# An encoder block on one core: whole-width sums and a new load order in the opening, v stores from ScalarE's queue, and another order of key evictions at the switch of heads

## The chip, the cores and the metric

The kernel runs on one core of one Trainium2 chip, in one launch. The metric is the device time of a launch in microseconds (us). Engines are called by their short names in the rows: PE is TensorE, PEld its weight loads, DVE VectorE, ACT ScalarE, POOL GpSimd, and SP SyncE, which here only issues transfers.

## What is computed

One encoder block on a sequence of 1024 positions with 1024 channels, in fp32. The conditioning vector c gives six vectors of shift, scale and gate through one matrix of 1024 x 6144:

```python
ada = jax.nn.silu(c) @ w_ada[i] + b_ada[i]
shift1, scale1, gate1, shift2, scale2, gate2 = [t[:, None, :] for t in jnp.split(ada, 6, axis=-1)]
h = rmsnorm(x, g_mix[i]) * (1 + scale1) + shift1
proj = h @ w_in[i]
qa, ka, va, qb, kb, vb, ga, gb = jnp.split(proj, split_at, axis=-1)
oa = mixture_of_dilations(heads(qa, N_HEADS_DIL), heads(ka, N_HEADS_DIL), heads(va, N_HEADS_DIL), rel_bias)
ob = neighbourhood_attention_2d(heads(qb, N_HEADS_NA), heads(kb, N_HEADS_NA), heads(vb, N_HEADS_NA), na_rpb[i])
merged = jax.nn.sigmoid(ga) * ya + jax.nn.sigmoid(gb) * yb
x = x + gate1 * (merged @ w_out[i])
```

`ya` and `yb` are oa and ob times a branch matrix each. Then follow a second norm, a feed-forward part with a depthwise convolution of width 3 and 2816 gated channels, and a final norm. There are eight dilated heads (three dilations each, merged by their denominators) and eight neighbourhood heads (a window of 8 x 16 on a grid of 16 x 64), all of width 64. The change touches the first norm, its modulation, the products for v, and the eviction of keys.

## The kernel before

**Products in three parts.** Every fp32 matrix product is made of three fp32r matmuls: an operand a is copied by ACT into its rounded high part, and DVE or POOL subtract that from a to give the low part. PE then adds high times high, high times low and low times high (`product`, L84 to L86). So each weight tile needs one ACT copy (`split`, L57) and one subtraction (L61), and each result that is used again as an operand needs both again: keys come out of PSUM as `ks` (ACT, L370) and `kl` (DVE, L374), softmax weights, transposed by PE into `T`, as `th` (ACT, L666) and `tl` (DVE, L667).

**The opening** (L437 to L530) is written in the order in which the engines are to run it; a manual schedule holds for all engines up to the attention. Positions go in two halves of 512; x of half 0 is loaded first. Its squares are summed over channel tiles on ACT and DVE (`total`, L452), and PE sums over the partitions by matmuls with a column of ones into `pcol` (`add_sums`, L98). DVE and ACT make r, the reciprocal root, of it; PE spreads r over the partitions into `pbc` (L111), and x is multiplied by it. At the same time comes the modulation of half of the channels that a "piece" needs: w_ada is loaded in columns of 512, each as four transfers of two row tiles. Of the eight row tiles, PE sums some directly by matmuls of one output column with c as the moving operand (`ada_sums`, L160, tile `pada`), and DVE accumulates the others (`ada_rows`, L174 and L176), with the accumulated rest summed by PE against ones. `piece_bias` (L293, L295) makes shift and scale of it; ACT then makes `h` (L229) and DVE its low part (L231). A loop over four pieces q of two channel tiles each does this and the products of one q and one k tile (`qk_products`, L310) and of v (`v_parts`, L320). Between the sums stand dummy matmuls on ones (`warm`, L236, out `pv`, in `om`), which compute nothing that is used.

**The v stage** (L538 to L606). For six further column groups of w_ada (j = 4 to 9) rows come in pairs (`pair_load`, L135, seven in flight); DVE sums them (L551, L553), and two steps later PE sums over partitions into `pada` and L167 adds the bias. Between these stand the v products, 128 positions by 512 columns each (`v_wide`, L279 to L281). A table `row_ends` says after which step how many pairs have been summed. `v_out` copies a product from PSUM on ACT (`vs`, two buffers, L286) and stores it to DRAM by a transfer on SP's queue (L287), from which the attention loads it again in another order. The first step without v products splits the v weights of the neighbourhood heads (L57, L61 with `vwh`, `vwl`).

**The attention** (L1074 to L1100) has 100 slots. Slots up to 63 hold turns of the dilated heads, from 64 on those of the neighbourhood heads. A slot runs on PE, in this order: O products (`th`, `tl` times v, L844), filler products of w_in (L84 to L86, one k step each), transposes T (L781, L827), filler, score products S, filler, W, filler. Each `fill` step also calls `catch_up(550)`, which hands out "asides" of a deque: evictions of the filler products, copies of v, splits. An aside is one or two closures with a cost; the first runs on ACT, the second on DVE, in an in-order stream of each engine. `k_evict` makes the asides of a key product: for a neighbourhood pair of heads one aside per head, ACT's copy `ks`, then DVE's `kl` (a cost of 750 for each). L658 and L659 are the two steps of the softmax (DVE, then ACT), L701 and L702 the eviction of O into `u`.

Transfers complete on eight semaphores that SP and ACT use in turn, so that the ninth issue waits until the first has landed.

Of the kernel before, what the change touches and what calls it, by code (L numbers as in the profile page):

```python
# [18 lines left out]
D = 1024  # L19
# [10 lines left out]
def hybrid_encoder(tc, xT, c, w_ada, small, w_in, p1_bias, p23_bias, na_bias, ln2_mult, ident, w_br, w_out,  # L30
# [62 lines left out]
    qkpool = tc.alloc_tile_pool(name="qk", bufs=4)  # L93

# [189 lines left out]
    def v_out(br, st, p, c0=0):  # L284
        vs = work.tile([128, 512], FT, name="vs", bufs=2)[:, :p.shape[-1]]
        act.activation(vs, p, AF.Copy)  # L286
        sp.dma_start((va_s, vb_c)[br][st * 128:st * 128 + 128, c0:c0 + p.shape[-1]], vs)  # L287
# [17 lines left out]
    def qk_products(ks):  # L305
        for k in ks:
            mhi, mlo = h[0, k]
            for x_, (part, m) in enumerate(((0, mhi), (1, mhi), (0, mlo))):
# [48 lines left out]
    def k_evict(br, qk, hf, p, later=at_once):  # L357
# [26 lines left out]
        for i in range(2 if br else 0):  # L384
            later(750, lambda i=i: one((i,)), lambda i=i: two((i,)))
# [33 lines left out]
    with tc.manual_schedule(engines={e.engine for e in (sp, act, dve, pool, pe)}):  # L419
# [5 lines left out]
        v_raw = [qkpool.tile([128, KT, 128], FT, name="kl") for _ in range(2)]  # L425
        half_load(v_raw, (8, 9), 0)
        wt.append(ada_load(1))
        half_load(qk_raw, (0, 4), 1)
        half_load(v_raw, (8, 9), 1)
        wt.append(ada_load(2))  # L430
# [15 lines left out]
        warm(35, idle, True)  # L446
# [6 lines left out]
        pcol = ps_n.tile([128, KT], FT, name="pcol")  # L453
        add_sums(pcol, total, True, True)
        warm(3, idle, True)
        pa = ada_sums([(wt[0][0], cs[:, 0:1])], stop=False)
        r = wpool.tile([128, KT], FT, name="rs", bufs=2)[:, :4]
        dve.tensor_scalar(r, pcol[:, :4], 1.0 / D, EPS, OP.mult, OP.add)
        act.activation(r, r, AF.Sqrt)
        ada_rows(wt[0], acc, range(3, 4), 3, 7)  # L460
# [3 lines left out]
        warm(3, idle, True)  # L464
        ada_sums([(wt[0][1], cs[:, 1:2])], pa, stop=False)
        warm(4, idle, True)
        ada_sums([(wt[0][2], cs[:, 2:3])], pa, stop=False)
        warm(2, idle, True)
        pbs = early.tile([128, 512], FT, name="mt", bufs=3)
        act.activation(pbs, pb, AF.Copy)  # L470
        ada_rows(wt[0], acc, range(4, 8), 3, 7)
        for k in range(2):
            dve.tensor_tensor(x[0][k], x[0][k], pb, OP.mult)
        ada_sums([(wt[0][7], ones)], pa)
        warm(5, idle, True)
        for q in range(4):
            ks = range(2 * q, 2 * q + 2)
            piece_bias(q, pa)
            if q == 0:
                for k in range(2, 4):  # L480
                    dve.tensor_tensor(x[0][k], x[0][k], pb, OP.mult)
                stage = [ps_n.tile([128, 512], FT, name=n) for n in ("pcol", "pbc")]
            low = [scaled(x[0][k], k) for k in ks]
            if q == 0:
                v_split(v_raw, (pool, pool), slice(0, 4), v_w[0])
                for k in range(4, 8):
                    pool.tensor_tensor(x[0][k], x[0][k], pbs, OP.mult)
# [4 lines left out]
            steps = (range(q + 1, 4), range(4, 5), range(5, 7)) if q else (range(0), range(2), range(2, 6))  # L492
# [5 lines left out]
            if q < 2:  # L498
                ada_rows(wt[q + 2], acc, range(q + 2), 0, 6)
# [6 lines left out]
            qk_products(ks)  # L506
# [1403 lines left out]
```

## Time and profile before

| What | us |
|---|---|
| three timed runs | 1501.80, 1496.16, 1500.61 |
| their median | 1500.61 |
| the profiled execution | 1498.67 |
| its span, first to last instruction | 1496.8 |
| PE busy | 1474.4 |
| DVE busy | 939.0 |
| ACT busy | 773.6 |
| POOL busy | 760.6 |

The rows of the profile are one execution; 1.87 us of its time lie outside of the span. The granted clock of PE was full (0.998 in the mean). A row of the timeline names start, duration, engine, line of the kernel, operation, the tile written and those read, and in brackets the idle time of the engine just before it and what ended that. A matmul on plain fp32 (sums, dummies, transposes of r) is recorded as two.

### The profile page before, as it was taken

The numbers are of one execution on the slowest core, as the hardware profiler recorded it, in microseconds if no ns is written. First come the engines' busy times: TensorE is split into PE (matmuls) and PEld (weight loads), VectorE is DVE, ScalarE is ACT, GpSimd is POOL, SyncE is SP. The second block draws the span as 40 slices with busy tenths as digits, with TensorE's granted clock in tenths as the row PEclk, the third lists the DMA queues.
The fourth block names the chain that finished last, engine by engine and source line by source line (L and its number), as shares of the span: only waits on it lengthen the run. The fifth ranks groups of instructions, "written<-read, shape, count | busy, mean of one in ns | idle before, by whom it ended". The sixth has DMA issues, their size and how long they took to land.

```text
span 1496.8 us, 21659 instructions
## 1 busy us (share of the span) xinstructions
PE 1474.4 (98%) x7664; PEld 1251.9 (84%) x7664; DVE 939.0 (63%) x1763; ACT 773.6 (52%) x1442; POOL 760.6 (51%) x633
## 2 busy tenths in 40 slices
PE   9999999999999999999999999999999999999997
PEld 8888888889798998888888778888888888877887
DVE  7683446465555665556515897666666667886865
ACT  4531666666655666653345464444444447474542
POOL 3031332434234454512268668766666776978811
PEclk9999999999999999999999999999999999999999
DMA  9577332444645555577544313222222233542313
GB/s 371 183 277 268 88 99 68 143 114 129 170 144 145 144 160 166 172 243 260 194 153 143 104 43 141 85 85 85 85 83 84 71 136 116 197 148 64 104 41 113
DMA packets 117301, 210.29 MB, mean 140 GB/s; under 512 B 42788, under 2 KB 55716, under 8 KB 117156
## 3 DMA queue, kind: packets, MB, share of 16 engines
q1 hardware_dynamic: 116632, 208.57, 43.4%
q8 instruction: 60, 0.98, 0.3%
q14 instruction: 49, 0.40, 0.1%
q10 hardware_dynamic: 560, 0.33, 0.1%
HBM read 163.58 MB, written 42.66 MB: 138 GB/s over the span
## 4 chain that ended last, share of the span: by engine, by line
PE 81%; DVE 5%; POOL 5%; DMA 4%; issue 2%; ACT 2%; SPq 0%; DVEq 0%; POOLq 0%; ACTq 0%
PE pj L84 10%; PE pj L86 10%; PE pj L85 10%; PE pj L1308 10%; PE pj L1307 10%; PE pj L1306 10%; PE pj L402 3%; PE O L1013 2%; DMA wraw<-w_down 2%; PE T L1000 1%; PE S L978 1%; POOL wsl L61 1%; PE pv L279 1%; PE pv L281 1%; PE pv L280 1%
## 5 line engine op out<-in xcount | busy, mean ns | idle before, releaser
L61 POOL TENSOR_TENSOR wlo<-wraw,whi 128x512 fp32r<-128x512 f32 (+1 forms) x84 | 106.1, 1284 | 144.8 <-ACT whi L57 129.8
L84 PE MATMUL pj<-h,whi 128*128 128x512 f32 x432 | 178.1, 412 | 0.4 <-DVE kl L374 0.4
L86 PE MATMUL pj<-h,wlo 128*128 128x512 f32 x432 | 169.8, 393 | 0.0
L85 PE MATMUL pj<-h,whi 128*128 128x512 f32 x432 | 169.4, 392 | 0.0
L1306 PE MATMUL pj<-op,wsh 128*128 128x512 f32 x408 | 159.1, 391 | 3.7 <-ACT wsh L57 2.7
L1307 PE MATMUL pj<-op,wsh 128*128 128x512 f32 x408 | 159.1, 390 | 0.9 <-DVE op L1237 0.6
L1308 PE MATMUL pj<-op,wsl 128*128 128x512 f32 x408 | 157.8, 390 | 0.7 <-POOL wsl L61 0.7
L667 DVE TENSOR_TENSOR tl<-T,th 128x512 fp32r<-128x512 f32 (+3 forms) x120 | 77.2, 654 | 101.2 <-ACT th L666 99.9
L717 POOL TENSOR_TENSOR wlo<-wraw,whi 128x512 fp32r<-128x512 f32 x58 | 74.4, 1293 | 126.8 <-ACT whi L716 126.7
L61 POOL TENSOR_TENSOR wsl<-big,wsh 128x512 fp32r<-128x512 f32 (+1 forms) x86 | 111.7, 1320 | 42.5 <-ACT wsh L57 37.6
L659 ACT ACTIVATE P<-P,st 128x256 f32<-128x256 f32 x128 | 64.2, 503 | 93.9 <-DVE st L658 93.9
L1543 DVE SCALAR_TENSOR_TENSOR big<-pj,sm,big 128x512 f32<-128x512 f32 (+2 forms) x183 | 94.9, 563 | 16.5 <-ACT big L1537 15.6
L86 PEld LDWEIGHTS pj<-h,wlo 128*128 128x128 f32 x432 | 81.1, 188 | 18.0
L1306 PEld LDWEIGHTS pj<-op,wsh 128*128 128x128 f32 x408 | 76.6, 188 | 21.9 <-ACT wsh L57 4.0
L1307 PEld LDWEIGHTS pj<-op,wsh 128*128 128x128 f32 x408 | 76.6, 188 | 18.2 <-DVE op L1237 1.2
L1308 PEld LDWEIGHTS pj<-op,wsl 128*128 128x128 f32 x408 | 76.6, 188 | 17.4 <-POOL wsl L61 1.8
L84 PEld LDWEIGHTS pj<-h,whi 128*128 128x128 f32 x432 | 81.5, 189 | 11.5 <-issue 0.8
L1308 PE MATMUL pj<-op,wlo 128*128 128x512 f32 x232 | 90.3, 389 | 0.0
L1307 PE MATMUL pj<-op,whi 128*128 128x512 f32 x232 | 90.3, 389 | 0.0
L1306 PE MATMUL pj<-op,whi 128*128 128x512 f32 x232 | 90.3, 390 | 0.0
L85 PEld LDWEIGHTS pj<-h,whi 128*128 128x128 f32 x432 | 81.7, 189 | 10.1
L61 POOL TENSOR_TENSOR wsl<-wraw,wsh 128x384 fp32r<-128x384 f32 (+1 forms) x46 | 57.3, 1268 | 62.1 <-ACT wsh L57 54.5
(398 smaller groups left out, 4173.6 us busy)
## 6 DMA issues: line engine op xcount, KB each, us to landing
wraw<-w_in SPq DMA_DIRECT2D x32, 512.0 KB
wada<-w_ada SPq DMA_DIRECT2D x31, 512.0 KB
big<-w_up SPq DMA_DIRECT2D x22, 512.0 KB
wraw<-w_up SPq DMA_DIRECT2D x22, 512.0 KB
big<-as SPq DMA_DIRECT2D x22, 512.0 KB
as<-big SPq DMA_DIRECT2D x21, 512.0 KB
gs<-gs SPq DMA_DIRECT2D x32, 256.0 KB
g<-gs SPq DMA_DIRECT2D x16, 512.0 KB
```

The source lines that it names most:

```text
L61: lo_eng.tensor_tensor(lo[:, i:i + step], raw[:, i:i + step], f(hi)[:, i:i + step], OP.subtract)
L84: pe.matmul(psum, whi[:, k0 + k], mhi, start=k == 0, stop=False)
L85: pe.matmul(psum, whi[:, k0 + k], mlo, start=False, stop=False)
L86: pe.matmul(psum, wlo[:, k0 + k], mhi, start=False, stop=k == n - 1)
L402: pe.matmul(p[:, 256 * r:256 * r + 256], ww[:, k], m[:, r], start=k + x + r == 0, stop=k == KT - 1 and x == 2, skip_group_check=True)
L659: act.activation(pp, pp, AF.Exp, bias=mi, scale=-1.0, accum_out=li)
L667: dve.tensor_tensor(tl[:m, :n], pt[:m, :n], f(th)[:m, :n], OP.subtract)
L717: pool.tensor_tensor(lo[:, i:i + n], raw[:, i:i + n], f(hi)[:, i:i + n], OP.subtract)
L1306: pe.matmul(psum, whi[:, k], bhi, start=j < 4 and k == 0, stop=False, skip_group_check=True)
L1307: pe.matmul(psum, whi[:, k], blo, start=False, stop=False, skip_group_check=True)
L1308: pe.matmul(psum, wlo[:, k], bhi, start=False, stop=k == n - 1, skip_group_check=True)
L1543: dve.scalar_tensor_tensor(y[:, dst], src, wt, y[:, dst], OP.mult, OP.add)
```

## The change

1. *Sums of the opening.* `add_sums` and `ada_sums` of pieces 0 and 1 are replaced by `wide_sums`: the moving operand is a column spread over 128 columns, and the result fills 128 columns, of which `every` reads the first. Row tile 1 of column 0 is handed to PE in the same call as row 0; row 3 of column 1 is summed by PE, no longer by DVE, in a gap of the first piece's products, which are now issued in parts. The dummies between the sums go, three are added ahead of them, and four stand behind them for five.
2. *Order on DVE and POOL.* Row 3 of column 0 is accumulated before r's first step, row 4 before its reciprocal. x tiles 2 and 3 are multiplied by POOL, not DVE. One row of column 3 goes from piece 1 to piece 2.
3. *Loads.* w_ada column 1 is issued ahead of the first half of the v weights, column 2 ahead of the second halves of the q, k and v weights.
4. *The v stage.* `v_out` there issues its store from ACT's queue. The loop that is interleaved with the rows runs one step further, so that sums of the last groups stand one step of v products later on PE.
5. *The attention.* In slots 53 to 57 the first filler hands out no asides; they are caught up with behind the T jobs.
6. *`k_evict` of neighbourhood heads.* The first aside is the first head's copy; the second aside holds the second copy and then both low parts.

PE at the beginning, before (`om` is the tile of ones that the dummies read, `kl`, `qs` and `wada` hold rows of w_ada, `pada` gets their sums):

```order
L236 MATMUL pv<-om 128x128 x35
L98 MATMUL pcol<-ones,sq 128x1 x4
L236 MATMUL pv<-om 128x128 x3
L160 MATMUL pada<-cs,kl 128x1 x4
L111 MATMUL pbc<-idt,rs 128x128 x4
L236 MATMUL pv<-om 128x128 x3
L160 MATMUL pada<-cs,kl 128x1 x4
L236 MATMUL pv<-om 128x128 x4
L160 MATMUL pada<-cs,qs 128x1 x4
L236 MATMUL pv<-om 128x128 x2
L160 MATMUL pada<-ones,qs 128x1 x4
L236 MATMUL pv<-om 128x128 x5
```

The same place of the changed kernel, up to the sums of column 1 (the numbers of the lines are its own):

```order
L246 MATMUL pv<-om 128x128 x38
L99 MATMUL pcol<-ones,sq 128x128 x4
L99 MATMUL pada<-cs,kl 128x128 x8
L121 MATMUL pbc<-idt,rs 128x128 x4
L99 MATMUL pada<-cs,qs 128x128 x4
L99 MATMUL pada<-ones,qs 128x128 x4
L246 MATMUL pv<-om 128x128 x4
L321 MATMUL pj<-h,whi 128x512 x2
L321 MATMUL pj<-h,wlo 128x512 x2
L99 MATMUL pada<-cs,wada 128x128 x4
L321 MATMUL pj<-h,whi 128x512 x4
```

The 12 dummies between the sums are gone, and four sums of column 1 stand inside the first tile's products.

ACT at the switch of heads, slots 53 to 56, before (`ks` are key copies, `th` the high parts of transposed weights, `P,st` a softmax, `vv` and `whi` copies for later products):

```order
L659 ACTIVATE P,st<-P,st 128x256 x2
L370 ACTIVATE ks<-pj 64x2x256 x2
L666 ACTIVATE th<-T 128x384
L624 ACTIVATE vv<-vv 128x8x64
L659 ACTIVATE P,st<-P,st 128x256 x2
L624 ACTIVATE vv<-vv 128x8x64
L701 ACTIVATE u_3684<-O 64x512
L666 ACTIVATE th<-T 128x512
L659 ACTIVATE P,st<-P,st 128x256 x2
L370 ACTIVATE ks<-pj 64x2x256 x2
L666 ACTIVATE th<-T 128x512
```

and after:

```order
L673 ACTIVATE P,st<-P,st 128x256 x2
L381 ACTIVATE ks<-pj 64x2x256
L680 ACTIVATE th<-T 128x384
L381 ACTIVATE ks<-pj 64x2x256
L638 ACTIVATE vv<-vv 128x8x64
L673 ACTIVATE P,st<-P,st 128x256 x2
L638 ACTIVATE vv<-vv 128x8x64
L715 ACTIVATE u_3677<-O 64x512
L680 ACTIVATE th<-T 128x512
L673 ACTIVATE P,st<-P,st 128x256 x2
L381 ACTIVATE ks<-pj 64x2x256
L680 ACTIVATE th<-T 128x512
```

Each `th` now stands between the two copies and no longer behind both; on DVE the two `kl` stand together behind `tl`, where `tl` stood between them.

The diff:

```diff
@@ -92,6 +92,16 @@
     ps_g = tc.alloc_tile_pool(name="psg", bufs=2, space=PSUM)
     qkpool = tc.alloc_tile_pool(name="qk", bufs=4)
 
+    def wide_sums(dst, blocks, col, first=False):
+
+        for m in range(4):
+            cc = slice(m * 128, m * 128 + 128)
+            pe.matmul(dst[:, cc], blocks[:, cc], col.to_broadcast([128, 128]), start=first and m == 0, stop=False,
+                      skip_group_check=True)
+
+    def every(p):
+        return p.rearrange("p (t c) -> p t c", c=128)[:, :, 0]
+
     def add_sums(pcol, sq, first, last, n=4):
 
         for t in range(n):
@@ -281,10 +291,10 @@
                 pe.matmul(p, hlo, whi, start=False, stop=k == KT - 1)
         return ps
 
-    def v_out(br, st, p, c0=0):
+    def v_out(br, st, p, c0=0, queue=sp):
         vs = work.tile([128, 512], FT, name="vs", bufs=2)[:, :p.shape[-1]]
         act.activation(vs, p, AF.Copy)
-        sp.dma_start((va_s, vb_c)[br][st * 128:st * 128 + 128, c0:c0 + p.shape[-1]], vs)
+        queue.dma_start((va_s, vb_c)[br][st * 128:st * 128 + 128, c0:c0 + p.shape[-1]], vs)
 
     sig = wpool.tile([128, KT], FT, name="rs", bufs=2)
     def piece_bias(q, pa):
@@ -302,10 +312,11 @@
         for raw, (hi, lo), e in zip(qk_raw, qk_w, lo_eng):
             split(raw[:, 4 * i:4 * i + 4], hi[:, 4 * i:4 * i + 4], lo[:, 4 * i:4 * i + 4], e)
 
-    def qk_products(ks):
+    def qk_products(ks, parts=range(3)):
         for k in ks:
             mhi, mlo = h[0, k]
-            for x_, (part, m) in enumerate(((0, mhi), (1, mhi), (0, mlo))):
+            for x_ in parts:
+                part, m = ((0, mhi), (1, mhi), (0, mlo))[x_]
                 for p, w in zip(qk_psum, qk_w):
                     pe.matmul(p, w[part][:, k], m, start=k + x_ == 0, stop=k == KT - 1 and x_ == 2)
 
@@ -381,8 +392,9 @@
                         sp.dma_start(f(t)[b], f(t)[a])
         if br == 0:
             later(1500, one, two)
-        for i in range(2 if br else 0):
-            later(750, lambda i=i: one((i,)), lambda i=i: two((i,)))
+        else:
+            later(750, lambda: one((0,)))
+            later(750, lambda: one((1,)), two)
 
     def q_blocks(qk, i):
         q = qkpool.tile([128, S], FR, name="qb", bufs=2)
@@ -423,11 +435,11 @@
         qk_raw = [wpool.tile([128, KT, 128], FT, name="wraw") for _ in range(2)]
         half_load(qk_raw, (0, 4), 0)
         v_raw = [qkpool.tile([128, KT, 128], FT, name="kl") for _ in range(2)]
+        wt.append(ada_load(1))
         half_load(v_raw, (8, 9), 0)
-        wt.append(ada_load(1))
+        wt.append(ada_load(2))
         half_load(qk_raw, (0, 4), 1)
         half_load(v_raw, (8, 9), 1)
-        wt.append(ada_load(2))
         wt.append(ada_rows_load(3))
         x.append(x_load(1))
         v_raw1 = [qkpool.tile([128, KT, 128], FT, name=n) for n in ("kl", "qs")]
@@ -443,73 +455,75 @@
 
         act.activation(sig, cs, AF.Sigmoid)
         dve.tensor_tensor(cs, cs, sig, OP.mult)
-        warm(35, idle, True)
+        warm(38, idle, True)
         total = early.tile([128, 512], FT, name="sq", bufs=2)
         for k in range(KT):
             sq = early.tile([128, 512], FT, name="mt", bufs=3) if k else total
             act.activation(sq, x[0][k], AF.Square)
             if k:
                 dve.tensor_tensor(total, total, sq, OP.add)
-        pcol = ps_n.tile([128, KT], FT, name="pcol")
-        add_sums(pcol, total, True, True)
-        warm(3, idle, True)
-        pa = ada_sums([(wt[0][0], cs[:, 0:1])], stop=False)
+        pcol = ps_n.tile([128, 512], FT, name="pcol")
+        wide_sums(pcol, total, ones, True)
+        pa = ps_s.tile([128, 512], FT, name="pada", bufs=1)
+        for t in range(2):
+            wide_sums(pa, wt[0][t], cs[:, t:t + 1], t == 0)
         r = wpool.tile([128, KT], FT, name="rs", bufs=2)[:, :4]
-        dve.tensor_scalar(r, pcol[:, :4], 1.0 / D, EPS, OP.mult, OP.add)
+        ada_rows(wt[0], acc, range(3, 4), 3, 7)
+        dve.tensor_scalar(r, every(pcol), 1.0 / D, EPS, OP.mult, OP.add)
         act.activation(r, r, AF.Sqrt)
-        ada_rows(wt[0], acc, range(3, 4), 3, 7)
+        ada_rows(wt[0], acc, range(4, 5), 3, 7)
         dve.reciprocal(r, r)
         qk_split(0, (pool, pool))
         pb = bcast(r, ps_n, "pbc")
-        warm(3, idle, True)
-        ada_sums([(wt[0][1], cs[:, 1:2])], pa, stop=False)
-        warm(4, idle, True)
-        ada_sums([(wt[0][2], cs[:, 2:3])], pa, stop=False)
-        warm(2, idle, True)
+        wide_sums(pa, wt[0][2], cs[:, 2:3])
         pbs = early.tile([128, 512], FT, name="mt", bufs=3)
         act.activation(pbs, pb, AF.Copy)
-        ada_rows(wt[0], acc, range(4, 8), 3, 7)
+        ada_rows(wt[0], acc, range(5, 8), 3, 7)
         for k in range(2):
             dve.tensor_tensor(x[0][k], x[0][k], pb, OP.mult)
-        ada_sums([(wt[0][7], ones)], pa)
-        warm(5, idle, True)
+        wide_sums(pa, wt[0][7], ones)
+        warm(4, idle, True)
         for q in range(4):
             ks = range(2 * q, 2 * q + 2)
-            piece_bias(q, pa)
+            piece_bias(q, pa if q > 1 else every(pa))
             if q == 0:
-                for k in range(2, 4):
-                    dve.tensor_tensor(x[0][k], x[0][k], pb, OP.mult)
                 stage = [ps_n.tile([128, 512], FT, name=n) for n in ("pcol", "pbc")]
             low = [scaled(x[0][k], k) for k in ks]
             if q == 0:
                 v_split(v_raw, (pool, pool), slice(0, 4), v_w[0])
-                for k in range(4, 8):
+                for k in range(2, 8):
                     pool.tensor_tensor(x[0][k], x[0][k], pbs, OP.mult)
             if q == 1:
                 qk_split(1, (pool, pool))
                 v_split(v_raw, (pool, pool), slice(4, 8), v_w[0])
             last = 6 if q else 5
-            steps = (range(q + 1, 4), range(4, 5), range(5, 7)) if q else (range(0), range(2), range(2, 6))
+            steps = (range(2, 4), range(4, 5), range(5, 7)) if q else ((), (0,), (1, 2, 4, 5))
             for some, then in zip(steps, low + [None]):
                 if q < 3:
                     ada_rows(wt[q + 1], acc, some, 0, last)
                 if then:
                     then()
             if q < 2:
-                ada_rows(wt[q + 2], acc, range(q + 2), 0, 6)
+                ada_rows(wt[q + 2], acc, range(2), 0, 6)
             if q == 2:
                 accs = sq_accs()
                 square(x[1], accs, range(4), dve)
             if q == 3:
                 v_split(v_raw1, (dve, pool), slice(0, KT), v_w[1])
                 square(x[1], accs, range(4, 8), dve)
-            qk_products(ks)
             if q == 0:
-                pa = ada_sums([(wt[1][t], cs[:, t:t + 1]) for t in (6, 7)], stop=False)
+                qk_products((0,), range(2))
+                pa = ps_s.tile([128, 512], FT, name="pada", bufs=1)
+                wide_sums(pa, wt[1][3], cs[:, 3:4], True)
+                qk_products((0,), range(2, 3))
+                qk_products((1,))
+                for t in (6, 7):
+                    wide_sums(pa, wt[1][t], cs[:, t:t + 1])
                 v_parts(0, range(4), ks, (0,))
-                ada_sums([(wt[1][5], ones)], pa)
+                wide_sums(pa, wt[1][5], ones)
                 v_parts(0, range(4), ks, (1, 2))
                 continue
+            qk_products(ks)
             v_parts(0, (0,), ks, range(3))
             if q < 3:
                 pa = ada_sums([(wt[q + 1][7], cs[:, 7:8])], stop=False)
@@ -537,7 +551,7 @@
         for t, raw in enumerate(v_raws[1]):
             sp.dma_start(raw, w_in[22 + t])
         v_steps = [(0, 4, 5), (0, 6), (0, 7), None] + [(1, st) for st in range(8)]
-        row_ends = (4, 7, 10, 12, 14, 17, 19, 22, 24)
+        row_ends = (4, 7, 10, 12, 14, 17, 19, 22, 24, 24)
         sums = {}
 
         def row_pairs(n0, n1):
@@ -575,7 +589,7 @@
 
         done_rows = 0
         due = {}
-        for n, step in enumerate(v_steps[:9]):
+        for n, step in enumerate(v_steps[:10]):
             if step is None:
                 for ks in (slice(0, 4), slice(4, 8)):
                     for hv in range(2):
@@ -595,7 +609,7 @@
             row_pairs(done_rows, row_ends[n])
             if step is not None:
                 for st, pp in zip(step[1:], p):
-                    v_out(step[0], st, pp)
+                    v_out(step[0], st, pp, queue=act)
             for j in due.pop(n, ()):
                 ada_bias(4 * j, ada_sums([(sums.pop(j), ones)]))
             due[n + 2] = [j for j in range(4, 10) if done_rows < 4 * j - 12 <= row_ends[n]]
@@ -626,7 +640,7 @@
         return vv
 
     first_w = w_split(ahead.pop(1), pool)
-    for br, st in v_steps[9:]:
+    for br, st in v_steps[10:]:
         v_out(br, st, *v_wide(st))
     work.release()
     ps_s.release()
@@ -1076,14 +1090,16 @@
     at(52, "first", vb_chunks)
     steps = fill_steps()
 
-    def fill(n):
+    def fill(n, asides=True):
         for _ in range(n):
             next(steps, None)
-            catch_up(550)
+            if asides:
+                catch_up(550)
 
     def run(jobs):
         return [job(*args) for job, args in jobs]
 
+    late_slots = range(53, 58)
     att = contextlib.ExitStack()
     att.enter_context(tc.manual_schedule(engines={e.engine for e in (pe, act, dve)}))
     for s in range(100):
@@ -1092,9 +1108,11 @@
         run(slots[s]["O"])
         if s == 99:
             break
-        fill(n // 4)
+        fill(n // 4, s not in late_slots)
         for job in run(slots[s]["T"]):
             job()
+        if s in late_slots:
+            catch_up(550)
         fill(n // 4)
         run(slots[s]["late O"])
         run(slots[s]["S"])
```

## The prediction

> **What bounds the kernel now.** I read the page's shares first, then TensorE's list of waits, because a kernel that keeps one engine full can only be shortened by that engine's work or its gaps.
>
> ```profile
> span 1496.8 us, 21659 instructions
> ...
> PE 1474.4 (98%) x7664; PEld 1251.9 (84%) x7664; DVE 939.0 (63%) x1763; ACT 773.6 (52%) x1442; POOL 760.6 (51%) x633
> ```
>
> TensorE is busy for 98% of the span, and no other engine comes near. The change takes no product away, so all that it can win is time in which TensorE waits, or fills time with dummy matmuls that compute nothing. The dummies count as busy, so the page hides them. The waits that the change aims at are these (total us, times, longest):
>
> ```profile
> PE O L844 <- ACT th L666: 1.5, 2, 0.9
> ...
> PE T L781 <- DVE tl L667: 0.9, 1, 0.9
> ...
> PE O L844 <- DVE tl L667: 0.7, 2, 0.4
> ...
> PE pada L160 <- DVE ada L167: 0.5, 1, 0.5
> ...
> PE pj L84 <- DVE kl L374: 0.4, 1, 0.4
> ...
> PE pv L279 <- ACT vs L286: 0.3, 1, 0.3
> ```
>
> Together 4.3 us, of which 3.1 (the first three rows) lie at the switch of heads, slots 53 to 57. The opening's dummies come on top. So the whole prize is below 1% of the span before any working.
>
> **The opening, first piece.** The timeline (start, duration, engine, line, then the idle time just before and what ended it):
>
> ```profile
> 11.30 1.05 PE L98 MATMUL pcol<-ones,sq 128*128 128x1 f32 x8 [0.24 <-DVE sq L452]
> ...
> 15.73 1.14 PE L236 MATMUL pv<-om 128*128 128x128 f32 x8
> 18.04 0.95 PE L160 MATMUL pada<-ones,qs 128*128 128x1 f32 x8
> 20.29 0.73 PE L310 MATMUL pj<-h,whi 128*128 128x512 f32 x2
> ...
> 12.39 0.16 DVE L458 TENSOR_SCALAR rs<-pcol 128x4 f32<-128x4 f32 x1 [1.14 <-PE pcol L98]
> 12.47 0.75 DVE L174 TENSOR_SCALAR pv<-qs,cs 128x512 f32<-128x512 f32 x1
> 16.47 1.29 DVE L473 TENSOR_TENSOR ks<-ks,pbc 128x512 f32<-128x512 f32 x2
> 19.03 0.16 DVE L293 TENSOR_TENSOR ada<-pada,sm 128x4 f32<-128x4 f32 x1 [1.28 <-PE pada L160]
> ...
> 19.42 0.81 ACT L229 ACTIVATE h<-ks,ada,am 128x512 fp32r<-128x512 f32 x1 [2.99 <-DVE am L295]
> ```
>
> L236 is the dummies: between the mean square and the row at 18.04 four groups of them (3, 3, 4 and 2 matmuls, two records each) stand between the sums. The modulation sum ends at 18.99, VectorE has waited 1.28 for it, ScalarE 2.99, and the first product follows 1.26 behind L293. A wide group (eight records of 128x128, 1.14) costs 0.19 more than a narrow one (0.95); with the dummies gone, TensorE would finish by about 16, ahead of VectorE. So VectorE sets the time: row 3 now fills its wait before L458, from 11.25 to 12.0; the mean square (its sums about 0.1 later, since three more dummies stand ahead of them and the wait there was 0.24) gives 12.5, row 4 runs to 13.3, the reciprocal to 13.4, rows 5 to 7 (three of 0.75, and a little between them) to about 15.8, the two x products (1.29) to 17.14. L293 stands behind them and no longer waits: 17.15 against 19.03, and the first product at 18.4 against 20.29, **1.9 earlier**. If row 3's load has not landed at 11.25, r comes behind it and up to 0.8 of this is lost.
>
> **The opening, later pieces.**
>
> ```profile
> 30.11 0.73 PE L310 MATMUL pj<-h,whi 128*128 128x512 f32 x2
> 38.77 0.74 PE L310 MATMUL pj<-h,whi 128*128 128x512 f32 x2 [0.47 <-ACT h L229]
> 52.59 0.28 PE L267 MATMUL pv<-vwh,h 128*128 128x256 f32 x1
> ...
> 27.32 0.75 DVE L174 TENSOR_SCALAR pv<-wada,cs 128x512 f32<-128x512 f32 x1 [0.60 <-DMA wada<-w_ada]
> 28.77 0.15 DVE L293 TENSOR_TENSOR ada<-pada,sm 128x4 f32<-128x4 f32 x1
> 36.79 1.02 DVE L295 SCALAR_TENSOR_TENSOR am<-ada,sm 128x2 f32<-128x2 f32 x1
> ...
> 35.27 2.53 POOL L61 TENSOR_TENSOR vwl<-kl,vwh 128x512 fp32r<-128x512 f32 x2
> ```
>
> Piece 1's modulation stands behind rows of the next column, of which one waited 0.60 for its load (27.32). That column now loads ahead of two weight halves, row 3 of column 1 is off VectorE (0.76), and so are two x products (1.28, the size of L473). TensorE pays four wide matmuls (about 1.1) for row 3, put where products waited for h. L293 of piece 1 then comes near 26.3 for 28.77, the products at 27.95 for 30.11: 2.2 earlier. In piece 2, VectorE's rows rather than TensorE led up to 38.77; the lighter VectorE brings another 0.7, so 35.9, **2.9 earlier**. Piece 3 and the tail add little; I put the end of the opening at 49.6 for 52.59, **−3.0**. The moved x products cost GpSimd two operations of 1.26 (half of L61's 2.53) behind its first low parts; x[2] is needed only for piece 1, and the idle time of GpSimd covers them. SP issues no load more; v half 0 and the second halves stand up to 2 MB later, which at 390 GB/s (the row under rival C) is some 5 us; the products read them only at the end of piece 0 and in piece 2. Bounds: −1.3 if only the wait at 19.03 goes; −4.4 if every wait above and VectorE's saved 2 us arrive in full.
>
> L295 at 36.79 took 1.02 for a 2-column operation and ended with GpSimd's L61 (35.27+2.53=37.80). By the Trainium skill, "SBUF — State Buffer", section "SBUF: two separate sides", VectorE with two SBUF inputs and a GpSimd operation that reads SBUF exclude each other through one shared port pair, for the whole instruction; the trace agrees at this row. By it, the x products moved to GpSimd could hold an L295 on the path by one whole operation, 1.26, and the opening would give −1.7 rather than −3.0 for each so held.
>
> **Around 131 us.**
>
> ```profile
> 131.19 0.50 PE L279 MATMUL pv<-vwh,h 128*128 128x512 f32 x1 [0.26 <-ACT vs L286]
> 134.01 1.02 PE L160 MATMUL pada<-ones,sq 128*128 128x1 f32 x8 [0.47 <-DVE ada L167]
> ...
> 94.35 1.17 ACT L286 ACTIVATE vs<-pv 128x512 f32<-128x512 f32 x2 [12.45 <-DMA v<-vs]
> 95.41 1.14 ACT L57 ACTIVATE vwh<-wraw 128x512 fp32r<-128x512 f32 x2
> ...
> 101.35 1.75 POOL L61 TENSOR_TENSOR vwl<-ks,vwh 128x512 fp32r<-128x512 f32 x1
> ...
> 103.66 0.39 PE L280 MATMUL pv<-vwl,h 128*128 128x512 f32 x1
> ```
>
> The two sums of row groups 8 and 9 move one step, 15 v products, back; at 0.22 each (45 in 10 us, the row under rival C) that is 3.3 us, more than the 0.5 and 0.3 that they waited. The stores of v are now issued by ScalarE right behind its copy, so SP's row loads no longer stand between copy and store. I take **−0.8**; zero if the landing itself is what was late; the rows have no more to give, and a loss is rival D. What was hidden: the split of the second v weights on ScalarE began at 95.41, GpSimd ended the last low part at 103.10, and TensorE used it at 103.66, so 0.56 of slack, and TensorE now comes 3.0 earlier. What hides the split is thus an earlier start: ahead of it ScalarE waited 12.45 for a store to land (94.35) that SP had issued behind loads. With the stores issued at once I expect it several us earlier, though four issues now stand ahead of it on ScalarE itself.
>
> **The switch of heads.**
>
> ```profile
> 379.19 1.08 ACT L370 ACTIVATE ks<-pj 64x512 fp32r<-64x512 f32 x1
> 381.44 1.08 ACT L370 ACTIVATE ks<-pj 64x512 fp32r<-64x512 f32 x1 [1.17 <-DVE kl L374]
> 392.40 1.06 ACT L370 ACTIVATE ks<-pj 64x512 fp32r<-64x512 f32 x1 [1.15 <-DVE kl L374]
> 393.48 0.60 ACT L666 ACTIVATE th<-T 128x512 fp32r<-128x512 f32 x1
> ...
> 384.77 0.42 DVE L658 CUSTOM_DVE_ANT_0 P<-S,bias 128x256 f32<-128x256 f32 x1
> 394.84 1.11 DVE L374 SCALAR_TENSOR_TENSOR kl<-pj,ks 64x512 fp32r<-64x512 f32 x1
> 395.98 0.42 DVE L658 CUSTOM_DVE_ANT_0 P<-S,bias 128x256 f32<-128x256 f32 x1
> 398.58 0.69 DVE L667 TENSOR_TENSOR tl<-T,th 128x512 fp32r<-128x512 f32 x1 [1.22 <-ACT th L666]
> ```
>
> Before, the order was ks, kl, ks, th, tl, kl, and ScalarE idled 1.17 and 1.15 between the copies. Now th (0.49 or 0.60) stands between the copies, and both kl (1.1 each) behind. From 379.19: ks to 380.27, th to 380.8, ks to 381.8, kl to 382.9 and 384.0, softmax L658 at 384.0 for 384.77. In the next evict, ks 390.06 to 391.1, th to 391.7 (for 393.48), ks to 392.7, kl to 394.9, L658 at 394.9 for 395.98. So the two turns of the O products come in time, but the chain ks, ks, kl, kl still runs serially ahead of the next softmax, and only 1.1 shorter. The next th and tl follow it, tl ending at 398.1 for 399.2, and the transposes T L781 that now wait 0.9 for tl wait for it again, longer. I take **−1.1**; zero if the kl's delay eats it, −3.1 if all three rows go; a loss is left out, as the same operations run behind one another with less idle time.
>
> The later neighbourhood evictions keep the two copies together:
>
> ```profile
> 449.82 1.09 ACT L370 ACTIVATE ks<-pj 64x512 fp32r<-64x512 f32 x1 [1.36 <-DVE kl L374]
> ```
>
> The second copy's 1.36 of waiting goes, the second kl ends 0.4 sooner, and the wait of pj L84 with it: **−0.4**, bounds 0 and −0.4.
>
> **The sum.** −3.0 −0.8 −1.1 −0.4 = −5.3. The profiled execution took 1498.67 with the span 1496.8 and 1.87 around it: 1493.4. The three timed runs lie from 1496.16 to 1501.8, median 1500.61, 1.9 over the profiled one, which would give 1495.3. I take 1494.0, between the two.
>
> **The rivals.**
> B, the whole switch is repaired: T L781 finds its buffer free because tl L667 moved ahead of u on VectorE. Then −3.0 −0.8 −3.1 −0.4 = −7.3, with the opening's best −8.7: 1491.4 to 1490.0, I say 1490.5. For it: the three rows are exactly the work reordered. Against: the serial chain above. 0.22.
> C, the opening's gain does not arrive: the transfers are full,
>
> ```profile
> 90.00:100.00 10.00, 10.00 (x45) 8.26 (x44) 7.14 (x10) 5.34 (x10) 3.31 (x3) 1.00 1.02 390
> ```
>
> and 1.02 of 16 engines' time between 90 and 100 (the next to last number) means that rows come when the loads come, not when TensorE is earlier. Stalls of 2 to 3 us then appear at sums of rows or at v products, and −5.3 becomes −2.3 to −3. The same comes of it if the L295 on the path are held as the one at 36.79 was, 0.86 more than its neighbour L293, two or three times: 1496 to 1497. The Trainium skill, "DMA: Bandwidth & Descriptors", section "Issuing engines are not separate DMA queues", says that ScalarE's issue saves only the sequencer's time, since all transfers interleave on the same engines; no row before shows a v store issued by ScalarE. By it the term at 131 would be 0 as well, and the time 1497.5. 0.17.
> D, slower: ScalarE runs in order, so a v store whose issue waits behind the saturated row loads holds the split of the second v weights. With TensorE 3.0 earlier, the split must begin by 95.41 + 0.56 − 3.0 = 93.0; each us later is a us of stall at L280, and from 98.3 on the sum is a loss. Beginning at 103 it gives 1498.67 − 5.3 + 10 = 1503.4. For it: the same loads; against: the stores before waited behind SP's row of loads, and now do not. 0.06.
>
> **How the numbers follow.** Forecast 0.55, B 0.22, C 0.17, D 0.06. Half a per cent, about what a measurement of this kernel can tell from no change, is 7.5 us, so faster starts below 1493.1: B, and a tenth of the forecast's own spread, 0.27; slower is D, 0.06; same 0.67. The range goes from B's best, 1490.0, less 2.5 (the profiled run lies that far above the fastest timed one), 1487.5, to past C, 1500.0; D is left out.
>
> **What would show it.** Right: the first product at about 18.4, L293 without a wait, the last product of the opening at 49.6; no wait of pada L160 for L167; at 394 no wait of O, but one of T L781 of some 2 us near 397. B would show TensorE without a gap between 388 and 402; C, waits for wada between 60 and 130; D, a gap at L280's first low part. I am wrong if v products in piece 0 or 2 wait for the weight halves that were put back, if wide sums cost clearly more than 1.14 a group, or if L295 grows.

## The result and the profile after

The changed kernel took 1492.05 us (median of six runs, 1490.45 to 1493.66) against 1500.16 of the kernel before in the same series: a ratio of 0.9948, 95% interval 0.9934 to 0.9962. A second series of the unchanged pair gave 0.9954 (0.9937 to 0.9971). So it is faster by 7 to 8 us, half a per cent; the forecast was 1494.0, with a sum of −5.3.

The page of the changed kernel: TensorE is busy for 2.9 us less (1474.4 before), so of the 8.2 us of span 5.3 are time in which it stood idle.

```profile
span 1488.6 us, 21635 instructions
...
PE 1471.5 (99%) x7652; PEld 1252.7 (84%) x7652; DVE 935.8 (63%) x1760; ACT 773.6 (52%) x1442; POOL 763.2 (51%) x635
```

Its opening in the timeline; lines of the changed kernel: sums L99, `piece_bias` L303 and L305, h L239, q and k products L321, first product after the pieces L277.

```profile
12.15 1.06 PE L99 MATMUL pcol<-ones,sq 128*128 128x128 f32 x8
...
19.22 0.73 PE L321 MATMUL pj<-h,whi 128*128 128x512 f32 x2 [0.67 <-ACT h L239]
...
28.55 0.63 PE L321 MATMUL pj<-h,whi 128*128 128x512 f32 x2
...
36.32 0.63 PE L321 MATMUL pj<-h,whi 128*128 128x512 f32 x2
...
49.60 0.28 PE L277 MATMUL pv<-vwh,h 128*128 128x256 f32 x1
...
17.97 0.15 DVE L303 TENSOR_TENSOR ada<-pada,sm 128x4 f32<-128x4 f32 x1
...
34.46 0.36 DVE L305 SCALAR_TENSOR_TENSOR am<-ada,sm 128x2 f32<-128x2 f32 x1
```

The end of the opening stands at 49.60 for 52.59. At the switch of heads (VectorE, TensorE, and the window's busy time, with clock, DMA share and GB/s as the last three numbers):

```profile
388.86 2.24 DVE L385 SCALAR_TENSOR_TENSOR kl<-pj,ks 64x512 fp32r<-64x512 f32 x2 [0.41 <-ACT ks L381]
391.12 0.42 DVE L672 CUSTOM_DVE_ANT_0 P<-S,bias 128x256 f32<-128x256 f32 x1
...
393.86 0.69 DVE L681 TENSOR_TENSOR tl<-T,th 128x512 fp32r<-128x512 f32 x1 [1.35 <-ACT th L680]
...
394.61 0.66 PE L795 MATMUL T<-idt,P 128*128 128x128 f32 x4 [2.51 <-DVE tl L681]
...
390.00:400.00 10.00, 7.49 (x33) 5.95 (x32) 6.63 (x19) 5.89 (x17) 2.12 (x2) 0.83 0.66 147
```

No O product waits any longer in this execution; the serial chain of low parts and softmax now ends in one wait of 2.51 for a transpose, and the granted clock is 0.83 in the mean of this window.

To sum over whole stages I take, for each pair of neighbouring matmuls, the time between their starts beyond what is usual for that pair (the median), where it is above 0.13 us; slower matmuls at a lower clock count too. Of the 8.2 us between the two spans:

| Stage | before | after | gained |
|---|---|---|---|
| end of the opening | 52.59 | 49.60 | 2.99 |
| around 131 us, waits | 1.05 | 0.00 | 1.05 |
| switch of heads, waits | 4.32 | 3.77 | 0.55 |
| later key eviction (454) | 0.57 | 0.22 | 0.35 |
| 820 to 900, untouched code | 3.08 | 3.57 | −0.49 |
| 1290 to 1400, untouched code | 4.96 | 1.08 | 3.88 |

The first four rows make 4.9, close to the forecast 5.3. The last row is what was not foreseen: waits for the operands of w_down in the down projection, where no line was changed. I call them the late waits.

### The profile page after: what moved, and what is told of

The parts are those of the page before. It is cut to its first block, busy times and chain, and to the rows that moved or that the text cites. A ratio compares the mean times of both kernels' runs of the same rounds, so it can differ in the third digit from the quotient of the medians.

```text
span 1488.6 us, 21635 instructions
## 1 busy us (share of the span) xinstructions
PE 1471.5 (99%) x7652; PEld 1252.7 (84%) x7652; DVE 935.8 (63%) x1760; ACT 773.6 (52%) x1442; POOL 763.2 (51%) x635
## 4 chain that ended last, share of the span: by engine, by line
PE 86%; DVE 4%; POOL 3%; DMA 2%; issue 2%; ACT 2%; SPq 0%; DVEq 0%; POOLq 0%; ACTq 0%
PE pj L1326 11%; PE pj L1325 11%; PE pj L1324 11%; PE pj L84 11%; PE pj L86 10%; PE pj L85 10%; PE pj L414 3%; PE O L1027 2%; PE T L1014 1%; PE S L992 1%; PE pv L289 1%; PE pv L291 1%; PE pv L290 1%; PE O L858 1%; PE O L807 1%
```

## The experiments

**What each part does alone.** Four kernels: the one before again, and before with one part of the change each, by the numbers of the list in the section on the change: 1 to 3 (opening), 4 (v stage), 5 and 6 (attention). Their diffs are these parts of the diff there.

> The kernel before, unchanged, for its spread and a second profile. In the two profiles at hand the local stages account for about 4.5 us (the opening 3.0, around 131 us 1.05, the switch of heads and the later eviction 0.4 together), and another 3.7 us lie between 1310 and 1390, where the matmuls wait for w_down loads, in code that the change leaves alone. Theory A (chance): the late waits differ from one execution to the next, so this second profile shows late waits nearer to the 1.1 us of after than to the 5.0 of before, and the ratio is 1.000 within 0.0015. Theory B (the change causes it): this profile shows about 5 us of late waits again. Ratio 1.000 by both.

> The opening's part alone (wide sums, load order, row order, x tiles 2 and 3 on POOL); the v stage and the attention as before. By the working of the opening: the last product of it 3.0 earlier, the waits around 131 us stay (1.05) unless the earlier arrival makes the second v weights late. Theory A: 0.9980 (-3.0 us), late waits unrelated. Theory B with the opening as cause of the late waits: 0.9955 (-6.7 us). The rival that the gain does not carry past the saturated loads: 0.9990 to 1.0000, with new waits between 60 and 135 us.

> The v stage's part alone (stores of v issued from ACT's queue, the loop with the rows one step longer). The two waits at 131 and 134 us go: -1.05 us, 0.9993. Theory B with the moved transfers as cause of the late waits (ten transfers fewer on SP's queue and ten more on ACT's): late waits of about 1 us rather than 5, and 0.9968 (-4.8 us). The rival that a store's issue holds ACT: 1.000 or above, with a wait where the second v weights are first used.

> The attention's two edits alone (no asides in the first filler of slots 53 to 57, both key copies before both low parts). From the profile after: the waits at the switch fall from 4.3 to about 3.8 us, all of it now at one transpose, and the one at 454 from 0.57 to 0.2: -0.5 to -1.0 us, 0.9994 to 0.9997. Theory B with this as the cause of the late waits: 0.9972 (-4.2 us) and late waits near 1 us.

Measured: control 0.9991 (0.9976 to 1.0005), opening 0.9965 (0.9949 to 0.9982), v stage 0.9986 (0.9969 to 1.0004), attention 0.9994 (0.9978 to 1.0009); the three parts add up to −8 us. This sum proves little: the control is the kernel before, and its median, 1498.72, lay 1.2 below the 1499.94 that the parts are compared with. Against the control's median the parts give −4.6, −0.7 and −0.1, together −5.4, and every interval is some 2.5 us wide to either side. What each of the opening's edits (sums, order, loads) gives alone was not tried. The profiles: both waits near 131 are gone with the v stage alone; the attention's part alone ends in a transpose wait of 3.6, and its waits at the switch add up to 5.1, more than the 4.3 of before. Late waits were 3.2 in the control, 3.3 and 4.0 with the v stage or the attention, 0.8 with the opening. So they did not vanish by mere repetition; something of the opening seemed to matter 1250 us later.

Looking there: SP issues two loads of w_down behind each other. The second of them in before, then in after, and DMA queue q8 in before from 1309 to 1312 (kind, packets, MB, share of the 16 DMA engines):

```profile
1310.31 1.57 SPq L1423 DMA_DIRECT2D wraw<-w_down  x1
```

```profile
1306.37 0.54 SPq L1441 DMA_DIRECT2D wraw<-w_down  x1
```

```profile
q8 instruction: 1, 0.02, 2.9%
```

I read q8 as the queue that loads TensorE's own program: its kind is "instruction", and it makes 60 loads of 16 KB in the span, one for some 128 matmuls. In the first four profiles with the old opening (before, control, vstage_only, attention_only) one of them began 0.6 to 0.8 us after the first issue, and the second issue took 1.16 to 1.57 instead of 0.54. With the new opening, whose program is six matmuls (in the balance of dummies and sums) shorter, it began 5 us behind the second issue.

**Is it the length of TensorE's program?** Dummies compute nothing, so six fewer in before, and six more in after, change that and, by 0.1 to 0.2 us, the end of the opening.

From before:

```diff
-        warm(35, idle, True)
+        warm(32, idle, True)
...
-        warm(5, idle, True)
+        warm(2, idle, True)
```

> The kernel before with six of its dummy matmuls in the opening left out (warm 35 to 32, and the last group 5 to 2, both where PE waits anyway), nothing else changed. The dummies compute nothing. Theory F (fetch): in the four profiles with the old opening a 16 KB load of PE's own program runs while SP issues the second w_down load near 1310 us, that issue takes 1.2 to 1.6 us instead of 0.55, and the waits between 1300 and 1400 us add up to 2.9 to 5.0; with the new opening PE's program is six matmuls shorter there, the 16 KB load falls about 5 us later, and the waits are 0.8 to 1.1. Six dummies less must do the same: the issue 0.55, late waits at most 1.5, 0.9975 to 0.9985 (-2.2 to -3.7 us). Rival C (chance, or something else in the new opening, its load order or its POOL work): the issue as slow as before, late waits 3 to 5, 1.000.

From after:

```diff
-        warm(38, idle, True)
+        warm(41, idle, True)
...
-        warm(4, idle, True)
+        warm(7, idle, True)
```

> The changed kernel with six dummies more (warm 38 to 41, and the last group 4 to 7), so that PE's program is as long as before. Theory F: the 16 KB load is back on SP's issue, late waits 2.9 to 5.0, the opening 0.7 to 1.0 later for the dummies: 0.9970 to 0.9980 of before. Rival C: only the 0.7 to 1.0 of the dummies, 0.9955.

The second issue in the one, and in the other:

```profile
1312.95 0.54 SPq L1423 DMA_DIRECT2D wraw<-w_down  x1
```

```profile
1306.34 1.02 SPq L1441 DMA_DIRECT2D wraw<-w_down  x1
```

The issue went both ways as the fetch theory says. The late waits, 0.5 and 4.8, went with it too, but in part by luck, as the table shows. The times decide nothing: 0.9991 (0.9975 to 1.0007), no faster than the control, and 0.9959 (0.9944 to 0.9974); each interval holds values of both theories. (The profiled execution of fetch_away also has a clock dip at 135 us, with waits of 3.4 there for 1.05; one execution does not explain a median of twelve.) Over all fourteen profiles ("second issue" and "S4" are durations, "S4" an operation explained below):

| Kernel | end of opening | second issue | S4 | late waits | span |
|---|---|---|---|---|---|
| before | 52.59 | 1.57 | 3.60 | 4.96 | 1496.8 |
| control | 53.92 | 1.24 | 3.57 | 3.18 | 1497.2 |
| vstage_only | 52.99 | 1.47 | 3.57 | 3.26 | 1494.7 |
| attention_only | 52.71 | 1.16 | 3.58 | 3.98 | 1496.5 |
| rows_step | 53.79 | 0.54 | 3.57 | 3.58 | 1497.5 |
| fetch_away | 52.67 | 0.54 | 1.35 | 0.52 | 1494.7 |
| opening_only | 49.65 | 0.54 | 1.35 | 0.79 | 1488.9 |
| after | 49.60 | 0.54 | 1.36 | 1.08 | 1488.6 |
| after_again | 49.53 | 0.54 | 3.56 | 3.40 | 1490.4 |
| fetch_back | 49.75 | 1.02 | 3.57 | 4.81 | 1494.7 |
| soft_first | 49.48 | 0.54 | 3.57 | 3.27 | 1490.1 |
| soft_late | 49.68 | 0.54 | 3.57 | 2.68 | 1490.7 |
| tuned | 49.41 | 0.54 | 1.35 | 0.72 | 1487.7 |
| s4_on_pool | 49.63 | 0.54 | on GpSimd | 1.33 | 1488.7 |

The slow issue comes with the long program (five of six) and never with the short one (none of eight). The sixth, rows_step, shows that the place of the load counts and not the length as such: there q8's load began at 1316.5, 5 us behind the second issue, and the issue took 0.54; why it came later there is open. But the slow issue is worth only about 0.7: the wait that follows it, near 1318 in before, is 0.9 to 1.1 with it and 0.3 in the mean without. The rest of the late waits goes with another column, S4.

**S4.** This is one VectorE operation of the down projection, the difference of two SBUF tiles of weights, next to GpSimd's low parts. In before (VectorE, then GpSimd):

```profile
1354.31 3.60 DVE L1273 TENSOR_TENSOR big<-wraw,big 128x384 f32<-128x384 f32 x1 [4.07 <-POOL wsl L61]
...
1354.25 1.99 POOL L61 TENSOR_TENSOR wsl<-wraw,wsh 128x384 fp32r<-128x384 f32 x2
1356.20 1.29 POOL L1381 TENSOR_TENSOR big<-big,wc 128x512 f32<-128x512 f32 x1
```

In after:

```profile
1348.24 1.36 DVE L1291 TENSOR_TENSOR big<-wraw,big 128x384 f32<-128x384 f32 x1 [3.17 <-POOL wsl L61]
...
1348.12 2.35 POOL L61 TENSOR_TENSOR wsl<-wraw,wsh 128x384 fp32r<-128x384 f32 x2
1350.43 1.30 POOL L1399 TENSOR_TENSOR big<-big,wc 128x512 f32<-128x512 f32 x1
```

In before S4 started 0.06 behind GpSimd and ended only 0.42 after three GpSimd operations were over (1356.20 + 1.29 = 1357.49); in after it came between the first two, which took 2.35 for 1.99. The next load of w_down waits for a buffer that S4 reads, so it is issued 2.2 us later, and TensorE waits 1.2 to 1.7 and 0.5 some 10 us behind. The Trainium skill, "SBUF — State Buffer", section "SBUF: two separate sides", has a VectorE instruction with two SBUF inputs and a GpSimd instruction that reads SBUF exclude each other for whole instructions; these rows agree, and they add that the loser may stay out for three instructions.

The changed kernel again, and with S4 on GpSimd:

```diff
-            dve.tensor_tensor(S4, a12, S2, OP.subtract)
+            (pool if apart else dve).tensor_tensor(S4, a12, S2, OP.subtract)
```

> The changed kernel, unchanged, for a second profile and a longer series. Of the 8.2 us between the two first profiles, 4.9 lie in the stages that the change touches and 3.3 in the waits after 1300 us. In ten profiles one VectorE operation of the down projection (S4, a difference of two SBUF tiles, 128x384) took either 1.36 us (three times) or 3.6 us (seven times), with GpSimd operations running beside it; the long one is followed by 2 us of waits at PE. Theory L (chance per execution): this profile may show it long, with late waits of 2.5 to 3.5 and a span of 1491; the series spreads over some 3 to 4 us. Theory P (fixed by the program): it is short again, late waits 1.1, span 1488.6. Ratio 0.994 to 0.996 by both.

> The changed kernel with the operation S4 of the down projection issued on GpSimd instead of VectorE, so that it can't stand against a GpSimd operation. Theory L or P with the shared access as the cause of the 3.6 us: no long one, no wait of about 2 us at PE near 1360, late waits at most 1.5, unless GpSimd, 1 us more loaded in each of twelve jobs, becomes late itself (new waits of PE for wsl between 1240 and 1480). 0.993 to 0.995 if GpSimd keeps up, above 0.996 if not.

The same program, another execution (after_again):

```profile
1348.02 3.56 DVE L1291 TENSOR_TENSOR big<-wraw,big 128x384 f32<-128x384 f32 x1 [2.43 <-POOL wsl L61]
```

So theory L holds as far as this: one and the same program shows both forms. Of the 3.88 between the first pair of profiles, 2.2 (the waits of 1.67 and 0.53 behind the long S4 of before) hang on it; between control and after_again the late waits differ by −0.2. What is not settled is whether the program shifts the odds. S4 was long in all five profiles with the slow issue and in four of the eight others, so the moved load may also bring the long form about; thirteen profiles can't tell that from chance. With S4 on GpSimd (1.02 each) there is no wait near 1360, late waits 1.3, and the six times lie within 1.5 us (1489.85 to 1491.39; after_again's eight within 6.4): 0.9943 (0.9924 to 0.9963), not to be told from after's 0.9954.

**The v stage.** Only the longer loop, the stores on SP's queue: part 4 of the change, but

```diff
-                    v_out(step[0], st, pp, queue=act)
+                    v_out(step[0], st, pp)
```

> Of the v stage's two edits only the longer loop; the stores of v stay on SP's queue. If the step of the sums alone removes the wait at 134 (0.63) and the stores' queue the one at 131 (0.42): 0.42 stays, 0.9996. If the stores on ACT's queue do nothing: both go, as in the run with both edits. If the earlier store is what keeps the second v weights in time: a new wait where they are first used.

0.9991 (0.9979 to 1.0004). The wait at 134 is gone, the one at 131 is there (TensorE; 1.4 us later in the span, as this execution's opening ended 1.2 later):

```profile
132.63 0.50 PE L279 MATMUL pv<-vwh,h 128*128 128x512 f32 x1 [0.45 <-ACT vs L286]
```

So each of the two edits removes one wait. Over all profiles the wait at 131 is there in five of the six with the stores on SP's queue (not in attention_only) and in none of the eight with them on ScalarE's. And the cover: the split of the second v weights begins at 96.94 here and at 91.46 in vstage_only, whose opening ended 0.8 earlier, so the stores' queue brings it some 4.7 forward. With the new opening it begins at 92.39 when the stores stay on SP's queue (opening_only, where no product waits for it either), and with them on ScalarE's, in after, at

```profile
87.85 1.15 ACT L57 ACTIVATE vwh<-wraw 128x512 fp32r<-128x512 f32 x2 [0.43 <-ACT vs L296]
```

**The switch.** From after, the softmax ahead of the low parts:

```diff
-        fill(n // 4)
+        fill(n // 4, s not in late_slots)
         run(slots[s]["late O"])
```

> The changed kernel with one edit more: in slots 53 to 57 the second filler hands out no asides either, so that on VectorE the softmax L672 stands ahead of the two low parts of keys and no longer behind them. If the serial chain of two copies and two low parts ahead of the softmax is what makes the transposes wait (2.5 us at L795, and slow matmuls behind it), the waits at the switch fall from 3.8 to below 1 us: 0.9948 becomes 0.992 to 0.993. If the transposes wait for another reason (the T job of the slot itself), no change: 0.9948.

Then also the weighing one slot later:

```diff
-                at(s0 + 24 + 2 * n, "last", self.weigh, g, z)
+                at(s0 + 24 + max(2 * n, 1), "last", self.weigh, g, z)
```

> The changed kernel with the softmax ahead of the low parts of keys in slots 53 to 57 (as in soft_first) and the first weighing of a merged pair (L933) one slot later. In soft_first the waits for transposes were gone, but VectorE stood 4.96 us in front of L933 for its factors to land, with the low parts of keys queued behind it, and PE waited 2.8 for those. If that queueing is the next limit: the waits at the switch fall from 3.8 to below 1 us and the ratio from about 0.9950 to 0.9925 to 0.9930. If the factors still land too late for the slot after: a wait of about 1 us there, 0.9940.

Then also four dummies fewer at the start:

```diff
-        warm(38, idle, True)
+        warm(34, idle, True)
```

> soft_late with four dummies fewer at the beginning (warm 34 for 38). In the profile after, the dummies ran up to the first sums at 12.15 with no wait, while the squares were ready by 11.4; so the opening should end 0.5 to 0.8 earlier: 0.0004 below soft_late. If the first sums wait for something else, no change.

Measured: 0.9948 (0.9929 to 0.9967), 0.9959 (0.9940 to 0.9977), 0.9965 (0.9952 to 0.9978). The chain theory was right as far as it went: the wait for transposes vanished in all three. But the time did not follow. TensorE's wait and its cause on VectorE in soft_first:

```profile
PE pj L84 <- DVE kl L385: 2.8, 1, 2.8
...
390.95 0.69 DVE L933 TENSOR_TENSOR u<-u,fb 128x512 f32<-128x512 f32 x1 [4.96 <-DMA fb<-fcs]
```

and in soft_late:

```profile
PE O L807 <- DVE tl L681: 4.0, 1, 4.0
...
411.87 0.69 DVE L933 TENSOR_TENSOR u<-u,fb 128x512 f32<-128x512 f32 x1 [6.50 <-DMA fb<-fcs]
```

L933 needs factors that come back from DRAM; one slot later it waited 6.50 for them instead of 4.96, and whatever stands behind L933 on VectorE waits with it. The wait only changed its place (4.3 at the switch in soft_first, 5.2 near 414 in soft_late, 4.8 in two places in tuned). Fewer dummies moved the sums from 12.15 to 11.47, and the opening's end from 49.6 to 49.41: 0.2 for the 0.5 to 0.8 expected.

**The clock in the old opening.** Control shows it: busy time in five microseconds of control, then of after (the granted clock is the third number from the end).

```profile
25.00:30.00 5.00, 5.00 (x30) 5.00 (x30) 3.51 (x7) 0.00 (x0) 5.00 (x5) 0.61 1.02 405
```

```profile
25.00:30.00 5.00, 4.95 (x37) 4.41 (x36) 4.46 (x9) 2.57 (x4) 5.00 (x5) 1.00 1.03 389
```

Three of the six profiles with the old opening, with its dummies and waits, have such a dip between 20 and 35 us, none of the eight with the new; two of the three end the opening at 53.8 to 53.9. So the old opening ends at 53.1 in the mean of six profiles, the new one at 49.6 in the mean of eight. What sets the dip off was not tried.

## Why the prediction was right, and where it was short

**The opening, −3.0: 2.99 measured.** The whole was right, the first piece was not, so that the agreement to 0.01 is luck. The three more dummies were put at 0.1, covered by a wait of 0.24; TensorE worked without a wait up to 12.15, 0.85 later than before. L303 came at 17.97 for the foreseen 17.15, the first product at 19.22 for 18.4. The later pieces gave it back: piece 1 at 28.55 (27.95 foreseen), piece 2 at 36.32 (35.9), the end at 49.60 (49.6), with 0.54 won behind piece 2, where the prediction put 0.1. The price that GpSimd's added operations could ask stayed small: L305 took 0.30 and 0.36 in pieces 1 and 2, not 1.02, and no product waited for it. What the sum lacked is the clock: against control the same edit gains 4.3, against the mean of the six profiles 3.5.

**Around 131, −0.8: 1.05.** Both waits are gone, each by its own edit; the reading under rival C, by which the stores' queue would bring nothing, did not hold. The split began at 87.85, before the limit of 93.0 (which 92.39, with the stores on SP's queue, would have met too), and rival D, ScalarE held by its stores, did not come up: its issues of stores took 0.33 to 0.35 each.

**The switch, −1.1: 0.55.** The mechanism was in the main as written: at 394 no wait of O, but one of T for tl, "some 2 us near 397" (2.51 at 394.61). The size fell short in two places: the wait of T is half a us longer than put, and of the two waits in the prediction's first row (O L844 for th) only the first is gone. The second, in before, then the same place in fetch_back:

```profile
401.71 0.33 PE L844 MATMUL O<-th,vv 128*128 128x128 f32 x1 [0.54 <-ACT th L666]
```

```profile
394.65 0.66 PE L795 MATMUL T<-idt,P 128*128 128x128 f32 x4 [2.49 <-DVE tl L681]
...
397.04 0.33 PE L858 MATMUL O<-th,vv 128*128 128x128 f32 x1 [0.55 <-ACT th L680]
```

In fetch_back the clock is full there, and the waits at the switch add up to 3.64. In after they add up to 3.77: its matmuls ran at a clock of 0.66 from 395 to 400 and filled the time in which O would have waited for th. So the low clock alone cost only about 0.1. Rival B, the switch repaired, did not happen, though the time lies near the one it gave. **At 454, −0.4: 0.35.** Rival C fell: no new wait between 60 and 131.

**The sum, −5.3 against −8.1 (−7 in the second series).** The intervals of the two series are 5.7 to 9.9 us and 4.3 to 9.4 us; the second holds the sum as it was, the first just misses it. The step that was short is the sum itself: it took the old opening and the stages that the change leaves alone as fixed, from one execution. They were not. The old opening ends 0.5 later in the mean than in the execution that was read, and about 0.7 comes with the moved load of TensorE's program; with the terms as measured that makes some 6. Of the late difference between the first two profiles 2.2 hang on the form of S4. That is luck of the pair if the two programs have the same odds, and this stays open: S4 was long in five of six profiles with the old opening and in four of seven with the new. The forecast time missed by 2.0 and not by 2.8 because its base, between the profiled execution and the median, lay 0.9 below the median of six.

## What to carry to other kernels

A difference between two profiles is first to be split by stage, and what lies in code that was not changed is to be looked for in a second profile of the same program before it is explained. Where waits hang on one chain (copies, low parts, softmax, then a round trip through DRAM), reordering one link moved the wait to the next link on the engine that runs in order. Slow matmuls behind a wait can hide another wait: what they cost is read from an execution without them. Dummies that keep TensorE busy also lengthen its program: here six of them shifted a load of it, 1250 us later, by some 5 us.

## What was not expected of the hardware

- When a load of 16 KB of TensorE's program ran at the same time, SP's DMA issue took 1.0 to 1.6 us instead of 0.54, in five of five profiles; in the nine others it took 0.54.
- A VectorE subtraction of two SBUF tiles took 3.6 us instead of 1.36 beside GpSimd operations that follow each other without a gap, in some executions of one program and not in others.
- A wait of 2.5 us of TensorE at the switch was followed by a granted clock of 0.66 over five microseconds in after, after_again and s4_on_pool, and by a full clock in fetch_back, where the same wait was 2.49.
